# Hybrid attention and SSD layer on one core: the division by the softmax sums moved behind the product with V, and a planner with a transfer limit and averaged times

## The chip, the cores and the metric

The kernel runs on one core of a Trainium2 chip, in one launch. A core has TensorE (PE, with its weight loads shown as PEld), VectorE (DVE), ScalarE (ACT), GpSimd (POOL) and SyncE (SP, which here only issues transfers), each with an instruction stream of its own that runs in order. The metric is the device time of one execution in microseconds (us). Three executions of the kernel before took 977.61, 975.49 and 984.52 us; the median is 977.61 us.

## The reference, cut to what matters

One layer: a modulated RMS norm, one input projection, then latent attention (16 heads) beside a bidirectional Mamba-2 SSD, one output projection, and a gated MLP. The change is about the attention of the latent queries:

```python
def attend(q_nope, q_rope, k_nope, k_rope, v):
    s = (jnp.einsum("bqhd,bkhd->bhqk", q_nope, k_nope)
         + jnp.einsum("bqhr,bkr->bhqk", q_rope, k_rope)) * ATTN_SCALE
    p = jax.nn.softmax(s.astype(jnp.float32), axis=-1).astype(v.dtype)
    return jnp.einsum("bhqk,bkhd->bqhd", p, v)
```

There are 512 latent queries and 768 keys (512 latent, 256 context), and V has 64 columns per head. The softmax divides every row of exponentials by its sum; the product with V is linear, so the division may come before it or after it.

## The kernel before, in words

**Numbers.** Every float32 operand of a large product is split into a high part (`act(..., AF.Copy)`, L498, on ScalarE) and a remainder (`tensor_tensor` subtract, L499, on VectorE), and each product is made of three passes on TensorE (high by high, high by low, low by high).

**Stages, in order of time.** The modulation and the z projection (L685); the other input projections with the depthwise convolution (L752, L787); the SSD of two head groups (L1006 to L1064) beside the attention's projections and, from about 285 us on, beside the attention itself; the attention alone; the output projection (L1299) from about 526 us; its norm and the transposes L1391 at about 600 to 625 us; the MLP's up projection (L752) and the down projection (L1531).

**One unit of attention.** `pair_of_heads(hp, ahead)` does two heads; of each head, four blocks of 128 queries. One block is a unit, 64 units in all. `scores` writes 128 x 768 scores to PSUM with six matmuls (L1176), VectorE takes the row maximum (L1178), ScalarE the exponential into SBUF with the row sum as a second output (L1180), VectorE the reciprocal of that sum, 128 x 1 (L1182), and GpSimd multiplies the 128 x 768 exponentials by it (L1183). Then `transposed` turns the six 128 x 128 blocks on TensorE (L1194), and both remainders and high parts of the transposed block are made by L498 and L499. After two units `weighted` makes the product with V in 24 matmuls (L1206) into the PSUM tile `po`. When a head is done, L1230 and L1231 add the two halves of `po` and write 64 of the 128 rows of `at`, the (value column x query) result of the pair. So in `at` a head is 64 partitions, and a query is a column.

**What else runs on the same engines.** GpSimd also has the SSD's products with per-head factors (L1006 and L1015 in the state steps, L1039, L1045, L1055, L1063), the query rotation (L1126, L1127) and the split of V (L1164). SyncE issues the loads of the weights (L490) and the copies that lay out queries and keys for both heads of a pair (L1151 to L1157). `modfinish` brings a 128 x 8 column table to a row on all partitions: transposed on VectorE (L1273), written to DRAM by four transfers (L1286), and read back by one broadcast (L1288).

**What sets the order.** The program is first written down once; `plan` then gives every instruction a price, simulates five engines and the transfers in `Graph.schedule`, chooses where each SBUF tile lies from the simulated starts and ends, and returns an order of the instructions of each engine, which is then fixed. `plan` repeats this: the starts and ends of one round choose the tiles' places of the next, and the round with the shortest simulated time is kept. A tile that takes the place of another waits for its users. The last four blocks of the output projection's 16 are done in a tail (`keep=4`), and the attention's results stand last in its order, the pair `hp = 7` as the sixteenth block.

## Time and profile before

| | us |
|---|---|
| median of 3 runs | 977.61 |
| profiled execution, its own time | 978.33 |
| its span (first to last instruction) | 976.5 |
| TensorE busy in the span | 952.8 |
| VectorE, ScalarE, GpSimd busy | 775.4, 538.9, 305.0 |
| first and last L1183 start | 294.0, 518.3 |

The span is the time from the first to the last recorded instruction; 1.8 us of the execution's own time lie around it. TensorE's matmuls are pipelined and the ends shown are modelled: a matmul of 512 columns is shown with about 390 ns, while the next one starts some 227 ns later. So a short gap between two matmuls shows as no idle time at all. The share of PEld, the weight loads, tells beside it how densely the matmuls stand.

### The profile page before, as it was taken

The page shows a single profiled execution, that of the slowest core. Times are in us where ns is not written, and L with a number is a line of the kernel's source. Part 1 is how long each engine was busy: PE and PEld are TensorE (multiplying, and loading weights), DVE is VectorE, ACT ScalarE, POOL GpSimd, SP SyncE. Part 2 cuts the span into 40 slices and gives each one's busy share as a digit, 9 for nine tenths or more (in the row PEclk, how much of TensorE's full clock was granted, in tenths as well). Part 3 has the DMA queues.
Part 4 walks back from the last instruction along what each step waited for, and adds up shares of the span by engine and source line. Part 5 has one row for each costly group of instructions (what it writes and reads, how often), then busy time and mean ns, then how long its engine had stood idle before and what let it go on. Part 6 is the DMA issues. An engine that isn't in the chain of part 4 may idle for free. (4 is left out here: it accounts for less than half of the span.)

```text
span 976.5 us, 14760 instructions
## 1 busy us (share of the span) xinstructions
PE 952.8 (98%) x5158; PEld 811.9 (83%) x5158; DVE 775.4 (79%) x1445; ACT 538.9 (55%) x1088; POOL 305.0 (31%) x273
## 2 busy tenths in 40 slices
PE   9999999999989999999999999899999999999995
PEld 8888888889867888898998888788888888887784
DVE  5799858997888999978889987955642542989998
ACT  4455327557669796698897223834412220457673
POOL 0001001874699978466541000000000052230021
PEclk7999999999999999999999999999999999999998
DMA  9913102001241233423487754426334323436784
GB/s 347 385 37 119 54 1 87 1 22 54 68 115 32 72 92 88 106 68 85 120 307 250 253 201 149 162 88 237 108 121 138 107 65 109 151 130 185 254 261 152
DMA packets 50234, 131.34 MB, mean 135 GB/s; under 512 B 6752, under 2 KB 9712, under 8 KB 50160
## 3 DMA queue, kind: packets, MB, share of 16 engines
q1 hardware_dynamic: 49360, 128.72, 41.0%
q10 hardware_dynamic: 800, 1.68, 0.5%
q8 instruction: 41, 0.67, 0.3%
q14 instruction: 33, 0.27, 0.1%
HBM read 110.43 MB, written 4.21 MB: 117 GB/s over the span
## 5 line engine op out<-in xcount | busy, mean ns | idle before, releaser
L752 PE MATMUL banks<-block,block 128*128 128x512 f32 (+1 forms) x2132 | 448.8, 361 | 3.4 <-DVE block L1395 2.0
L752 PEld LDWEIGHTS banks<-block,block 128*128 128x128 f32 x2132 | 358.0, 188 | 64.7 <-DVE block L1395 2.7
L498 ACT ACTIVATE block<-block 128x512 fp32r<-128x512 f32 (+4 forms) x340 | 215.4, 664 | 185.6 <-PE banks L752 48.2
L499 DVE TENSOR_TENSOR block<-block,block 128x512 fp32r<-128x512 f32 (+4 forms) x340 | 265.8, 816 | 50.4 <-PE banks L752 29.2
L1183 POOL TENSOR_TENSOR block<-block,smalls 128x768 f32<-128x768 f32 x64 | 97.1, 1526 | 49.6 <-DVE smalls L1182 32.4
L1531 PE MATMUL banks<-block,block 128*128 128x512 f32 x462 | 108.5, 390 | 1.3 <-DVE block L499 1.1
L1531 PEld LDWEIGHTS banks<-block,block 128*128 128x128 f32 x462 | 86.3, 188 | 21.1 <-DVE block L499 2.5
L1176 PE MATMUL banks<-block,block 128*128 128x512 f32 (+1 forms) x384 | 93.4, 351 | 3.2 <-ACT block L1180 1.7
L499 DVE TENSOR_TENSOR block<-banks,block 128x512 fp32r<-128x512 f32 (+1 forms) x156 | 83.7, 556 | 7.0 <-ACT block L498 5.4
L1299 PE MATMUL banks<-block,block 128*128 128x512 f32 x384 | 89.0, 390 | 0.0
L1299 PEld LDWEIGHTS banks<-block,block 128*128 128x128 f32 x384 | 71.9, 188 | 14.6
L498 ACT ACTIVATE block<-banks 128x512 fp32r<-128x512 f32 (+1 forms) x156 | 74.1, 499 | 16.4 <-PE banks L1194 7.4
L1206 PE MATMUL banks<-block,block 128*128 128x256 f32 x384 | 69.5, 297 | 0.2 <-ACT block L498 0.2
L1176 PEld LDWEIGHTS banks<-block,block 128*128 128x128 f32 x384 | 59.2, 189 | 10.4 <-ACT block L1180 3.5
L587 DVE SCALAR_TENSOR_TENSOR block<-block,block 128x1024 f32<-128x1024 f32 x52 | 62.5, 1219 | 4.9 <-DMA block<-in_wmod_dram 4.9
L1180 ACT ACTIVATE block<-banks,smalls 128x768 f32<-128x768 f32 x64 | 57.8, 904 | 15.5 <-DVE smalls L1178 9.4
L1194 PE MATMUL banks<-cst,block 128*128 128x128 f32 x384 | 63.8, 273 | 0.3 <-DVE block L499 0.2
L1178 DVE TENSOR_REDUCE smalls<-banks 128x1 f32<-128x768 f32 x64 | 60.8, 950 | 3.0 <-PE banks L1176 2.4
L1440 POOL TENSOR_TENSOR block<-block 128x256 f32<-128x256 f32 x11 | 10.4, 952 | 168.4 <-DVE block L1432 143.8
L787 DVE SCALAR_TENSOR_TENSOR block<-banks,cwh,block 128x510 f32<-128x510 f32 (+3 forms) x88 | 51.5, 620 | 12.4 <-ACT block L783 11.9
L1206 PEld LDWEIGHTS banks<-block,block 128*128 128x128 f32 x384 | 56.3, 189 | 4.2 <-ACT block L498 0.6
L1194 PEld LDWEIGHTS banks<-cst,block 128*128 128x128 f32 x384 | 46.8, 140 | 9.0 <-POOL block L1183 1.2
(231 smaller groups left out, 1134.3 us busy)
## 6 DMA issues: line engine op xcount, KB each, us to landing
block<-in_wdn_dram SPq DMA_DIRECT2D x99, 256.0 KB, 3.1
block<-in_wmod_dram SPq DMA_DIRECT2D x48, 512.0 KB, 4.8
block<-in_wup_dram SPq DMA_DIRECT2D x44, 512.0 KB, 3.6
block<-block SPq DMA_DIRECT2D x32, 256.0 KB, 3.1
block<-in_wout_dram SPq DMA_DIRECT2D x16, 512.0 KB, 5.0
block<-block SPq DMA_DIRECT2D x56, 128.0 KB, 2.5
block<-in_wxbc_dram SPq DMA_DIRECT2D x12, 512.0 KB, 4.3
block<-in_wz_dram SPq DMA_DIRECT2D x16, 256.0 KB, 7.3
```

What stands on the lines that cost most here:

```text
L498: act(hi, src, AF.Copy)
L499: (lo_eng or V).tensor_tensor(out=lo, in0=src, in1=hi, op=ALU.subtract)
L587: V.scalar_tensor_tensor(out=junk, in0=wt, scalar=0.5, in1=vec, op0=ALU.mult, op1=ALU.mult, accum_out=acc)
L752: mm(po, lhsT=wf(k, pt[0]), rhs=xf(k, pt[1]), start=(k == 0 and pt == parts[0]), stop=(k == nk - 1 and pt == parts[-1]))
L1176: mm(sc[:, o : o + n], lhsT=q_[:, x_, qi * P : (qi + 1) * P], rhs=kk[:, y_, :], start=part == 0, stop=part == 2)
L1178: V.reduce_max(nm, sc[:, :T], axis=AX.X, negate=True)
L1180: act(pe, sc[:, :T], AF.Exp, bias=nm, scale=1.0, accum_out=sm_)
L1183: G.tensor_tensor(out=pe, in0=pe, in1=sm_.to_broadcast([P, T]), op=ALU.mult)
L1194: nc.tensor.transpose((tx if c < NX else tc_)[:, o : o + P], pe[:, s_ : s_ + P], ident)
L1206: mm(po[:, half * 256 : half * 256 + 256], lhsT=vst(c), rhs=rhs, start=(part == 0 and c == 0), stop=(part == 1 and c == NKT - 1))
L1299: mm(po[i][:, nh * 512 : nh * 512 + 512], lhsT=l[lp][:, i * P : (i + 1) * P], rhs=w[wp][:, nh * 512 : nh * 512 + 512], start=(k == 0 and l ...
L1531: mm(po[i], lhsT=l[:, lp, i * P : (i + 1) * P], rhs=w[wp], start=first and q == 0 and n == 0, stop=q == PAIRS[-1] and n == 2, skip_group_c ...
```

## The change

**In the attention.** `scores` no longer makes the reciprocal (L1182) and no longer multiplies (L1183); what is transposed and multiplied with V are the bare exponentials. The 64 row sums now go to the columns of one tile per pair, `sums` (128 queries x 8 blocks). When both heads of a pair are done, one reciprocal of 128 x 8 is taken, `turned` (taken out of `modfinish`, which uses it too) transposes it on VectorE, four transfers of 8 x 32 elements write it to DRAM as 8 rows of 128, two transfers read four rows each back, each to 64 partitions, and one GpSimd product of 128 x 512 multiplies `at` by it.

**In the planner.** A transfer may not start, in the simulation, before the eighth last one has landed (`FLYING = 8`). The starts and ends that choose the tiles' places are now the mean of the last round's and the new ones. There are 24 rounds, before 16. `PACE = 1.0` only names a number that stood there.

```diff
-DMA_START, DMA_WAIT, DMA_AHEAD, DMA_ALONE, RUN = 650, 910, 3000, 0.8, 80
+DMA_START, DMA_WAIT, DMA_AHEAD, DMA_ALONE, RUN, FLYING = 650, 910, 3000, 0.8, 80, 8
...
-        ticks, held, port = {}, 0, 0.0
+        ticks, held, port, flying = {}, 0, 0.0, []
...
+            if self.dma[i] and not self.back and len(flying) >= FLYING:
+                t = max(t, flying[-FLYING])
...
+            if self.dma[i]:
+                flying.append(end[i] + DMA_WAIT + DMA_ALONE * self.cost[i])
...
-def plan(ins, pieces, hints, units, rounds=16):
+def plan(ins, pieces, hints, units, rounds=24):
...
-        took, order, start, end = Graph(full, eng, dma, cost, share, tables, urgent, opens, shared).best()
+        took, order, *now = Graph(full, eng, dma, cost, share, tables, urgent, opens, shared).best()
+        start, end = ([(p + q) / 2 for p, q in zip(*v)] for v in zip((start, end), now))
...
-    def scores(qkk, qi):
+    def scores(qkk, qi, sum_):
...
-        nm, sm_ = small("nm"), small("rs")
+        nm = small("nm")
         V.reduce_max(nm, sc[:, :T], axis=AX.X, negate=True)
         pe = t4(P, T)
-        act(pe, sc[:, :T], AF.Exp, bias=nm, scale=1.0, accum_out=sm_)
+        act(pe, sc[:, :T], AF.Exp, bias=nm, scale=1.0, accum_out=sum_)
         pfree(sc)
-        V.reciprocal(out=sm_, in_=sm_)
-        G.tensor_tensor(out=pe, in0=pe, in1=sm_.to_broadcast([P, T]), op=ALU.mult)
         return pe, ox, oc
...
+    def turned(w):
+
+        V.transpose(out=w[:, 1, :], in_=w[:, 0, :])
+        return [w[b * 32 : b * 32 + 8, 1, :] for b in range(4)]
+
...
+        sums, inv = t2(P, 2, 32), t2()
+        G.memset(sums[:, 0, 2 * NX :], 0.0)
+        back = nc.dram_tensor(f"sums_{hp}", (2 * NX, P), F32, kind="Internal").ap()
...
-                    transposed(*scores(heads[j], half * 2 + q2), pT, q2)
+                    transposed(*scores(heads[j], half * 2 + q2, sums[:, 0, j * NX + half * 2 + q2 :][:, :1]), pT, q2)
...
+        V.reciprocal(out=sums[:, 0, : 2 * NX], in_=sums[:, 0, : 2 * NX])
+        for b, piece in enumerate(turned(sums)):
+            nc.sync.dma_start(out=back[:, b * 32 : b * 32 + 32], in_=piece)
+        for j in range(2):
+            nc.sync.dma_start(out=inv[j * 64 : j * 64 + 64],
+                              in_=back[j * NX : j * NX + NX].rearrange("(o n) p -> o (n p)", o=1).to_broadcast([64, S]))
+        G.tensor_tensor(out=at, in0=at, in1=inv, op=ALU.mult)
```

TensorE has the same 4977 instructions before and now. VectorE loses 64 reciprocals and gains 8 reciprocals and 8 transposes, GpSimd loses 64 products and gains 8 memsets and 8 products, and SyncE gains 48 transfers. The order of all engines is planned anew. In the changed kernel's order the lines stand 6 higher up to L1176, 4 higher at L1194 and L1206, and 13 higher from L1299 on.

GpSimd, in the SSD's second group, where the decay blocks are made (L1039, now L1045) while attention units run. Before:

```order
L1039 TENSOR_TENSOR block_441_2775<-block_438_2754 128x256
L1183 TENSOR_TENSOR block_387_2529<-block_387_2529,smalls 128x768
L1039 TENSOR_TENSOR block_441_2775<-block_210_1511 128x256
L1045 TENSOR_TENSOR block_438_2754<-block_226_1599,hd 128x512
L1183 TENSOR_TENSOR block_422_2650<-block_422_2650,smalls 128x768
L1039 TENSOR_TENSOR block_441_2775<-block_438_2754 128x256
L1183 TENSOR_TENSOR block_138_806<-block_138_806,smalls 128x768
L1039 TENSOR_TENSOR block_442_2776<-block_210_1511 128x256
```

Now, at the same place:

```order
L1045 TENSOR_TENSOR block_443_2773<-block_427_2685 128x256
L1045 TENSOR_TENSOR block_443_2773<-block_274_1846 128x256
L1045 TENSOR_TENSOR block_443_2773<-block_427_2685 128x256
L1045 TENSOR_TENSOR block_443_2773<-block_274_1846 128x256
L1045 TENSOR_TENSOR block_444_2774<-block_427_2685 128x256
L1132 TENSOR_TENSOR block_274_1846<-block_274_1846,block_106_643 128x512
L1045 TENSOR_TENSOR block_444_2774<-block_274_1846 128x256
L1133 TENSOR_TENSOR block_274_1846<-block_274_1846,block_471_2972 128x512
```

The products with the sums are gone from between the SSD's instructions, and nothing of the attention's units is left on GpSimd there.

TensorE, at the end of the second group's state steps (L1011, now L1017), where the first units' scores (L1176, now L1182) begin. Before:

```order
L1176 MATMUL banks<-block_354_2357,block_201_1425 128x512
L1011 MATMUL banks<-block_43_307,block_208_1504 128x512
L1011 MATMUL banks<-block_43_307,block_209_1505 128x512
L1011 MATMUL banks<-block_59_391,block_208_1504 128x512
L1176 MATMUL banks<-block_29_234,block_201_1425 128x256 x3
L1011 MATMUL banks<-block_31_250,block_208_1504 128x512
L1011 MATMUL banks<-block_31_250,block_209_1505 128x512
L1011 MATMUL banks<-block_43_307,block_208_1504 128x512
L1176 MATMUL banks<-block_354_2357,block_201_1425 128x512 x3
```

Now:

```order
L1182 MATMUL banks<-block_113_674,block_73_460 128x512 x3
L1198 MATMUL banks<-cst,block_277_1899 128x128
L1017 MATMUL banks<-block_295_2001,block_208_1508 128x512
L1017 MATMUL banks<-block_295_2001,block_189_1296 128x512
L1017 MATMUL banks<-block_334_2285,block_208_1508 128x512
L1198 MATMUL banks<-cst,block_277_1899 128x128 x5
L1182 MATMUL banks<-block_356_2364,block_73_460 128x256 x3
L1182 MATMUL banks<-block_113_674,block_73_460 128x512 x2
L1017 MATMUL banks<-block_356_2364,block_208_1508 128x512
```

The first unit's transposes (L1194, now L1198) stood behind the last state product; now those of the first units stand between the state products, with 18 of these still to come when the first transpose is due.

SyncE, where the loads and copies for a coming pair are issued. Before:

```order
L490 DMA block_210_1511<-in_wqr_dram 128x384
L1156 DMA block_642_4149<-block_195_1370 64x1024
L1151 DMA block_72_445<-block_606_3875 64x512
L490 DMA block_616_3933<-in_wk_dram 128x256
L1157 DMA block_43_307<-block_43_307 64x512
L1156 DMA block_59_391<-block_195_1370 64x1024
```

Now, at the first returns of sums (pairs 0 and 2, whose writes alternate; pair 1 follows later):

```order
L1247 DMA sums<-block_210_1514 8x32
L1247 DMA sums<-block_398_2572 8x32
L1163 DMA block_553_3422<-block_43_307 64x512
L1247 DMA sums<-block_210_1514 8x32
L1247 DMA sums<-block_398_2572 8x32
L1249 DMA block_215_1522<-sums 64x512
L496 DMA block_398_2572<-in_wqr_dram 128x384
L1249 DMA block_215_1522<-sums 64x512
L1160 DMA block_611_3867<-block_483_3000 32x1024
L1157 DMA block_611_3867<-block_546_3407 64x1024
```

The writes of the sums and the reads that wait for them stand among the loads and copies for the next pair; behind the first read there stand a weight load and the layout copies. At the end of the output projection, from the sixteen transposes of the first two row blocks to the last four of the fourth, 50 products of the MLP stood between the transposes; now 69 do.

More of the change, by code (lines that the diff above doesn't have):

```diff
@@ L91 @@
 IDLE = 22, 13, 13
+PACE = 1.0
 class Memory:
@@ L1249, in build @@
     second = projections()
-    beside(group_sums(), second, 1.0)
+    beside(group_sums(), second, PACE)
     alone[0] = True
@@ L1266, in modblock @@
         moddot(wt, cs, mod[:, src * 8 + j : src * 8 + j + 1])
-    def row_pieces(ms):
-        w = t2(P, 2, 32)
-        G.memset(w[:, 0, 8:], 0.0)
-        G.tensor_copy(w[:, 0, :8], ms)
-        V.transpose(out=w[:, 1, :], in_=w[:, 0, :])
-        return w[:, 1, :]
     def modfinish(n, src, add, nrm, row=True):
@@ L1283, in modfinish @@
             return
-        turned = row_pieces(ms)
-        for b in range(4):
-            nc.scalar.dma_start(out=scratch[n][:, b * 32 : b * 32 + 32], in_=turned[b * 32 : b * 32 + 8])
+        w = t2(P, 2, 32)
+        G.memset(w[:, 0, 8:], 0.0)
+        G.tensor_copy(w[:, 0, :8], ms)
+        for b, piece in enumerate(turned(w)):
+            nc.scalar.dma_start(out=scratch[n][:, b * 32 : b * 32 + 32], in_=piece)
         row = t4()
```

## The prediction

> **What bounds the kernel now.** The page comes first, for the engines' shares.
>
> ```profile
> span 976.5 us, 14760 instructions
> PE 952.8 (98%) x5158; PEld 811.9 (83%) x5158; DVE 775.4 (79%) x1445; ACT 538.9 (55%) x1088; POOL 305.0 (31%) x273
> ```
>
> TensorE is busy for all but 23.7 us, and the change takes no instruction from it. So the most that any edit of the other engines can win is TensorE's waiting, and the next view must say where that is: the busy time by stage (columns: window, TensorE, weight loads, VectorE, ScalarE, GpSimd, granted clock, DMA share, GB/s).
>
> ```profile
> 0.00:150.00 150.00, 147.76 (x788) 128.69 (x788) 118.62 (x252) 64.13 (x103) 6.40 (x17) 0.95 0.43 157
> 526.00:600.00 74.00, 74.00 (x328) 61.27 (x327) 66.03 (x131) 22.17 (x28) 2.00 (x4) 1.00 0.71 244
> 600.00:625.00 25.00, 21.95 (x141) 19.20 (x140) 22.24 (x80) 18.14 (x49) 1.59 (x1) 1.00 0.51 169
> 625.00:875.00 250.00, 250.00 (x1204) 210.55 (x1204) 138.14 (x184) 83.92 (x120) 38.51 (x46) 1.00 0.37 124
> 875.00:976.50 101.50, 89.86 (x391) 72.59 (x389) 95.37 (x208) 63.79 (x139) 9.54 (x6) 0.97 0.64 207
> ...
> 150.00:293.00 143.00, 138.50 (x786) 116.06 (x784) 123.14 (x193) 94.39 (x209) 88.94 (x73) 1.00 0.20 56
> 293.00:526.00 233.00, 230.73 (x1531) 203.55 (x1532) 211.82 (x404) 192.38 (x446) 158.07 (x127) 1.00 0.39 110
> ```
>
> Nearly half of the idle time, 11.6 us, lies at the end, where the attention is long done, and 2.2 us at the start. The change can reach 4.5 us of 150 to 293, 2.3 us of 293 to 526 and 3.1 us of 600 to 625. Since a short gap shows as no idle time, the same view in finer steps, with a stretch of plain 512-column matmuls as a measure:
>
> ```profile
> 275.00:293.00 18.00, 14.35 (x64) 10.06 (x62) 15.58 (x22) 10.12 (x21) 15.67 (x14) 1.00 0.54 134
> 293.00:350.00 57.00, 55.04 (x343) 45.81 (x344) 52.72 (x92) 46.88 (x127) 52.97 (x45) 1.00 0.25 65
> 350.00:400.00 50.00, 49.99 (x305) 43.27 (x303) 48.82 (x99) 38.01 (x90) 37.24 (x31) 1.00 0.29 72
> 400.00:450.00 50.00, 49.70 (x341) 44.30 (x341) 42.72 (x90) 41.09 (x91) 31.16 (x26) 1.00 0.36 86
> 450.00:526.00 76.00, 76.00 (x549) 70.17 (x548) 67.56 (x126) 66.40 (x141) 36.70 (x27) 1.00 0.59 185
> ...
> 725.00:825.00 100.00, 100.00 (x443) 82.77 (x442) 39.03 (x52) 21.73 (x26) 21.55 (x28) 1.00 0.34 111
> ```
>
> Matmuls that follow each other without a wait keep the weight loads at 83% (725 to 825, wide matmuls) or up to 92% (450 to 526, attention alone, narrow ones). From 275 to 293 they stand at 56%, from 293 to 350 at 80%, then at 87 and 89%. At these two measures the loads of 275 to 293 need 10.06/0.828 = 12.2 us, so 5.8 us are lost; those of 293 to 350 need 49.6 to 55.3, so 1.7 to 7.4 are lost; those of 350 to 450 need 94.9 to 105.8 us of 100, so 0 to 5.1. Together 7.5 to 18.3 us are lost around the first units. There GpSimd is busy for 15.67 of 18 and 52.97 of 57 us, VectorE for 52.72 of 57 and 48.82 of 50. What TensorE waits for in the whole run, where it shows:
>
> ```profile
> PE banks L752 <- DVE block L1395: 2.0, 2, 1.0
> PE banks L1176 <- ACT block L1180: 1.7, 3, 0.9
> PE banks L1176 <- DMA block<-block: 1.5, 2, 1.2
> ```
>
> None of these is GpSimd by name: L1183 stands one step earlier, between a unit's exponential and its transposes.
>
> **The change part by part.** Removed, and the nearest rows to what is added:
>
> ```profile
> L1183 POOL TENSOR_TENSOR block<-block,smalls 128x768 f32<-128x768 f32 x64 | 97.1, 1526 | 49.6 <-DVE smalls L1182 32.4 <-DMA block<-in_wmod_dram 4.0 <-PE banks L1194 2.9
> L1182 DVE RECIPROCAL smalls<-smalls 128x1 f32<-128x1 f32 x64 | 9.4, 156 | 7.4 <-ACT block L1180 6.6
> L1055 POOL TENSOR_TENSOR block<-block,block 128x512 f32<-128x512 f32 x14 | 20.4, 1460 | 5.2 <-DVE block L1053 5.0
> L1271 POOL MEMSET block<- 128x24 f32 x3 | 0.4, 121 | 23.0 <-PE banks L1299 15.4 <-issue 7.6
> L924 DVE RECIPROCAL block<-block 128x192 f32<-128x192 f32 x1 | 1.3, 1346 | 0.0
> L1273 DVE STREAM_TRANSPOSE block<-block 128x32 f32<-128x32 f32 x3 | 0.6, 207 | 0.1
> L1286 ACTq DMA_DIRECT2D mod_rows<-block x12: 269/288/534, 566.6 to 800.8; - x12
> L1288 ACTq DMA_DIRECT2D block<-mod_rows x3: 349/350/353, 576.9 to 927.7; - x3
> block<-block SPq DMA_DIRECT2D x56, 128.0 KB, 2.5
> DMA to landing us min/median/max: 4.7/5.2/5.7
> ```
>
> *GpSimd.* It loses 64 x 1.526 = 97.1 us (its own durations; GpSimd spans are rough) and gains 8 x 1.46 (L1055 is the same shape) and 8 x 0.12, 12.7 us. In 293 to 526 it falls from 158 busy us to about 74. Of itself this is worth nothing: TensorE is the bound, and where other units fill it, the products were hidden. What it is worth is shorter waiting. A unit's way from exponential to transposes loses 0.156 + 1.526 us and, by L1183's idle row, 32.4/64 = 0.5 us of waiting for L1182: about 2.2 us per unit. And the state steps, whose L1006 and L1015 also run on GpSimd, can now be filled with whole units, since a unit needs no GpSimd: in the new order transposes stand between the state products. I take half of the 5.8 us of 275 to 293 (the other half belongs to the SSD's own chain and to the copies of queries and keys, the L1176 row above), 2.9. Of 293 to 350 I take the lower end, 1.7, and 1.0 for all above it, as VectorE stays at over 90% there. Bounds of these: 0, if the idle time is VectorE's, and 18.3.
>
> *VectorE* loses 9.4 us and gains 8 reciprocals of 128 x 8, not in the trace: between 0.156 (one column) and 1.346 (192), taken as 0.2, being near the first; and 8 x 0.207. Net some 6 us less of 212. Its work with both inputs in SBUF also runs beside a freer GpSimd:
>
> ```profile
> L499 DVE TENSOR_TENSOR block<-block,block 128x512 fp32r<-128x512 f32 x14 | 8.8, 687 | 0.0
> L499 DVE TENSOR_TENSOR block<-block,block 128x512 fp32r<-128x512 f32 x34 | 30.5, 900 | 3.5 <-ACT block L498 2.7 <-PE banks L1011 0.5
> ```
>
> The first row is 50 to 125 us, GpSimd nearly idle; the second 150 to 293, GpSimd 62% busy: 0.21 us more for each. This is VectorE time, and counted in the 1.0 above, not once more. Where one reciprocal now waits for the eighth sum, the row maxima behind it on VectorE wait with it: at most the 6.6 us that L1182 waited, in 8 places where it was 17, so nothing is charged.
>
> *The return of the sums.* SyncE gains 32 writes and 16 reads, 32 x 0.288 + 16 x 0.35 = 14.8 us of issuing (ScalarE's rows for the same forms), over some 300 us. A read waits for four writes; behind it stand a weight load and layout copies for the next pair (the order of SyncE). How long a 1 KB write takes to land no row says: at most 3.35 us, as L1288 was issued at 584.45, after its last write at 581.10, and below by nothing but the issue, 0.27.
>
> ```profile
> 581.10 0.27 ACTq L1286 DMA_DIRECT2D mod_rows<-block  x1
> ...
> 584.45 0.35 ACTq L1288 DMA_DIRECT2D block<-mod_rows  x1
> ```
>
> I take 2.5, the landing of the smallest common copy, for the write and 2.5 for the read of 128 KB. The Trainium skill, DMA: Bandwidth & Descriptors, section "Anatomy of one DMA — SWDGE (gpsimd) path", gives a transfer a fixed cost of about 2.0 us, most of it the receipt of the write and heaviest when it goes to HBM, which speaks against a return through DRAM; by it, an estimate from that page, the round trip would be some 4.3 us and the sum no other; the 2.5 us that a 128 KB copy takes here agrees with it. What hides it: nothing needs `at` before the output projection's last blocks. The cover of the last pair is shown by the 526 to 600 row: TensorE runs 74 us without idle time, and the pair is split for its sixteenth block. I charge 0; without the cover the last pair would cost 2.5 + 2.5 + 1.5, 6.5 us, once. On GpSimd the product with the sums waits for the read, and behind it stand splits of V (L1164) for later pairs. SyncE already waits longer than that, in 290 to 526, for what its transfers overwrite or read:
>
> ```profile
> SPq L490 <- PE banks L1194: 27.7, 7, 16.3
> SPq L1151 <- DVE block L499: 29.1, 14, 7.8
> ```
>
> *The planner's edits* move everything else. At 600 to 625, 69 products instead of 50 stand between the transposes.
>
> ```profile
> 616.14 2.43 PE L752 MATMUL banks<-block,block 128*128 128x256 f32 x18
> 618.42 0.60 PE L1391 MATMUL banks<-cst,block 128*128 128x128 f32 x4
> ```
>
> At (618.42 - 616.14)/18 = 0.127 us, 19 more fill 2.4 of the 3.1 idle us, if their operands are there; VectorE, at 22.24 of 25, makes those, so I take 1.0 (bounds 0 and 2.4). Start and end keep their orders but for a few rows: 0.
>
> *Sum:* 2.9 + 1.7 + 1.0 + 1.0 = 6.6 us. The profiled execution took 978.33 us, 0.7 above the median of the runs, 977.61; so 971.0 us.
>
> **The rivals.** About 1% is what a measurement of this kernel can tell from no change: 967.8 and 987.4 us are the bounds.
>
> *Hidden anyway.* The products lay beside TensorE's work, and VectorE, at 92 to 98% from 293 to 400, keeps the first units waiting; the new order loses elsewhere what it wins here. For it: 230.73 of 233 us are already busy. Against it: the weight loads at 56 and 80%. Time 975.5 to 981.
>
> *The whole of it.* All of 18.3 us and some of 2.4 come back, because GpSimd at 93% was what held 293 to 350. Time 977.6 - 18.3 - 1 = 958 at best, 966 at two thirds. For it: state steps and units no longer meet on any engine but VectorE. Against: VectorE.
>
> *Headroom in the weight loads.* They stand at 203.55 of 233 us in the attention; were the rest free, 29.5 us could go: 948. The 92% of 450 to 526 and the 83% of 725 to 825 with no idle time speak against it. The Trainium skill, Perfetto Trace Analysis, section "Identifying the Most-Contended Engine", says matmul busy time is a poor measure of headroom and to take the share of the weight loads; here a stretch without a wait stands at 83%, so the trace follows it only below that.
>
> *SyncE held.* A read of the sums stands at the head of SyncE until four writes land, and the copies of the next pair's queries and keys start late; L1176 then waits for "DMA block<-block", now 1.5 us. Price: 2.5 us (5.2 at the upper landing row) for each of 8 pairs, 20 to 42 us, less the 6.6 won: 991 to 1012; with half the pairs hit, 981. It decides from the point where copies reach SyncE's head less than 2.5 us before their scores. For it: the view shows such waits already. Against: SyncE's waits are for places and for L499, so its loads are mostly early.
>
> **How the numbers follow.** The forecast, 966 to 975.5, has 0.42, of which 0.10 below 967.8; hidden anyway 0.25, same; the whole of it 0.15, faster; headroom 0.03, faster; SyncE held 0.15, of which 0.12 above 987.4. Faster 0.10 + 0.15 + 0.03 = 0.28; slower 0.12; same 0.60. The range 961 to 983 leaves out headroom (0.03), a third of the whole of it (0.05) and most of SyncE held (0.12).
>
> **What would show it.** GpSimd near 220 us in all, no group of 128 x 768 on it; weight loads over 70% in the 18 us around the first scores and over 83% after; L499 of 128 x 512 from SBUF nearer to 687 ns there; 600 to 625 with 1 to 2 us idle. Wrong: VectorE's L499 as TensorE's releaser for more than now; L1176 waiting for copies for over 10 us; idle time in 526 to 600 (the return uncovered); or idle time moved to 875 to 925.

## The result, and the profile after

The changed kernel takes 973.0 us, the median of 20 executions (970.4 to 978.2), beside 977.51 us for the kernel before (20 executions, 975.49 to 984.52). The ratio is 0.995, with a 95% interval of 0.9935 to 0.9965. So the change wins 4.5 us, surely more than nothing and less than the 1% that was set as the bound of "same".

The page of the changed kernel:

```profile
span 976.4 us, 14657 instructions
PE 955.5 (98%) x5158; PEld 816.5 (84%) x5158; DVE 760.4 (78%) x1397; ACT 538.4 (55%) x1088; POOL 224.7 (23%) x225
```

GpSimd went from 305.0 to 224.7 busy us and VectorE from 775.4 to 760.4. But the two profiled spans are equal, 976.5 and 976.4, although the medians differ by 4.5 us. The reason stands in the first 50 us. The kernel before, busy time by window (TensorE, weight loads, VectorE, ScalarE, GpSimd, granted clock, DMA share, GB/s):

```profile
0.00:25.00 25.00, 22.91 (x128) 22.06 (x128) 13.37 (x40) 11.13 (x19) 1.10 (x8) 0.80 0.94 347
25.00:50.00 25.00, 25.00 (x143) 21.91 (x143) 20.33 (x45) 12.05 (x21) 0.00 (x0) 0.93 1.00 379
```

The changed kernel, the same windows:

```profile
0.00:25.00 25.00, 22.97 (x112) 22.41 (x113) 13.36 (x40) 10.89 (x19) 1.10 (x8) 0.70 0.94 344
25.00:50.00 25.00, 25.00 (x136) 22.17 (x135) 15.23 (x36) 7.46 (x13) 0.00 (x0) 0.82 0.87 315
```

The granted clock (third number from the right) was 0.80 and 0.93 in the one execution, 0.70 and 0.82 in the other. In clock time 25 x (0.20 + 0.07) = 6.8 us were lost before and 25 x (0.30 + 0.18) = 12.0 after, 5.2 us more. By then the changed kernel had also done 23 matmuls fewer (112 + 136 for 128 + 143), which at 227 ns each are 5.2 us too. So the profiled execution of the changed kernel, 978.2 us, is its longest of 20, and starts some 5 us behind. The stages behind the start can still be compared, if one keeps in mind that the changed kernel reaches them later.

The rest of the changed kernel by stage, same columns:

```profile
150.00:275.00 125.00, 124.17 (x723) 106.74 (x722) 111.13 (x178) 81.97 (x183) 69.85 (x61) 1.00 0.14 44
275.00:293.00 18.00, 17.32 (x94) 14.01 (x94) 13.50 (x19) 13.74 (x30) 15.81 (x14) 1.00 0.36 85
293.00:350.00 57.00, 55.82 (x361) 47.81 (x360) 52.36 (x91) 47.35 (x122) 35.52 (x35) 1.00 0.32 78
350.00:400.00 50.00, 49.67 (x301) 43.14 (x301) 43.20 (x90) 40.00 (x98) 19.90 (x21) 1.00 0.34 89
400.00:450.00 50.00, 50.00 (x341) 44.42 (x340) 38.35 (x75) 41.30 (x91) 10.39 (x15) 1.00 0.39 97
450.00:526.00 76.00, 75.11 (x531) 67.60 (x530) 68.26 (x115) 63.96 (x134) 10.57 (x12) 1.00 0.67 203
526.00:600.00 74.00, 74.00 (x328) 61.30 (x327) 60.98 (x123) 23.19 (x30) 8.80 (x4) 1.00 0.71 253
600.00:625.00 25.00, 23.61 (x157) 20.91 (x156) 23.35 (x77) 17.21 (x45) 1.29 (x1) 1.00 0.50 175
625.00:875.00 250.00, 250.00 (x1195) 210.23 (x1194) 139.76 (x188) 84.01 (x123) 39.41 (x46) 1.00 0.36 119
875.00:925.00 50.00, 47.83 (x207) 37.94 (x206) 47.92 (x96) 34.11 (x73) 0.00 (x0) 1.00 0.68 211
925.00:976.40 51.40, 40.05 (x177) 32.84 (x175) 45.80 (x110) 29.09 (x64) 8.91 (x6) 0.93 0.62 204
```

The two windows of the kernel before that the prediction does not show:

```profile
150.00:275.00 125.00, 124.16 (x724) 106.00 (x723) 107.56 (x172) 84.27 (x188) 73.27 (x60) 1.00 0.15 45
...
875.00:925.00 50.00, 48.66 (x210) 38.80 (x209) 48.83 (x98) 33.90 (x73) 0.00 (x0) 1.00 0.66 207
```

Both kernels have the same matmuls, so behind the start, where the granted clock is 1.00 in both up to 925 us, the weight loads are an account of work done. (Over the whole span the changed kernel has 4.6 us more of them, 816.5 for 811.9, at the same 5158 loads: those of the first 50 us lasted longer under its lower clock, 180 ns on average for 163, and the 23 that it had not done by 50 us come later.) After minus before, in us:

| stage | weight loads | TensorE idle |
|---|---|---|
| 150 to 275 | +0.74 | -0.01 |
| 275 to 293 | +3.95 | 3.65 to 0.68 |
| 293 to 350 | +2.00 | 1.96 to 1.18 |
| 350 to 526 | -2.58 | 0.31 to 1.22 |
| 526 to 600 | +0.03 | 0 and 0 |
| 600 to 625 | +1.71 | 3.05 to 1.39 |
| 625 to 875 | -0.32 | 0 and 0 |
| 875 to the end | -1.82 | 11.64 to 13.52 |

From 275 to 625 the changed kernel does 5.1 us more of loads in the same 350 us, and 0.7 from 150 to 275. At the rate of that stretch (299.19 us of loads in 350, 0.855) this is 5.8/0.855 = 6.8 us of time. At the end 1.9 us of waiting come back. That leaves 4.9, beside 4.5 by the medians.

What TensorE waits for in the whole of the changed kernel (us, times, longest):

```profile
PE banks L1544 <- DVE block L505: 2.2, 2, 1.5
...
PE banks L758 <- DVE block L1408: 0.7, 2, 0.5
PE banks L1182 <- DMA block<-block: 0.6, 1, 0.6
...
PE banks L1182 <- ACT block L1186: 0.3, 1, 0.3
```

The scores (L1176, now L1182) waited 1.7 us for the exponential and 1.5 for a copy; now 0.3 and 0.6. The transposes' copies (L1395, now L1408) held the MLP's products (L752, now L758) for 2.0 and now for 0.7 us. At the top now is the down projection (L1531, now L1544), waiting 2.2 us near the end for remainders made on VectorE (1.1 before).

What was added, by line (count, then ns min/median/max, first and last start):

```profile
L1245 DVE RECIPROCAL block<-block x8: 194/197/204, 313.7 to 522.8; 128x8 f32<-128x8 f32 x8
L1247 SPq DMA_DIRECT2D sums<-block x32: 267/336/738, 383.8 to 533.7; - x32
L1249 SPq DMA_DIRECT2D block<-sums x16: 450/510/597, 392.8 to 540.1; - x16
L1251 POOL TENSOR_TENSOR block<-block,block x8: 1286/1294/6458, 396.9 to 543.4; 128x512 f32<-128x512 f32 x8
```

And what these wait for in the changed kernel, first GpSimd's group (last part: its idle time ahead of the eight products), then SyncE from 290 to 560 us:

```profile
L1251 POOL TENSOR_TENSOR block<-block,block 128x512 f32<-128x512 f32 x8 | 16.6, 2079 | 80.1 <-DMA block<-sums 68.5 <-DMA block<-block 7.8 <-DVE block L1243 3.7
```

```profile
SPq L1157 <- DVE block L505: 26.0, 15, 7.1
...
SPq L1247 <- DVE block L1215: 12.4, 4, 8.7
...
SPq L1249 <- DMA sums<-block: 9.0, 4, 5.5
```

GpSimd stands 68.5 us ahead of six of the eight products until the sums are back, and SyncE stands 9.0 us until writes have landed. Neither shows on TensorE: 526 to 600 has no idle time, and the scores' wait for copies became shorter.

### The profile page after: what moved, and what is told of

Its sections match the earlier page's. It is cut to its first block, busy times and chain, and to the rows that moved or that the text cites. A ratio compares the mean times of both kernels' runs of the same rounds, so it can differ in the third digit from the quotient of the medians.

```text
span 976.4 us, 14657 instructions
## 1 busy us (share of the span) xinstructions
PE 955.5 (98%) x5158; PEld 816.5 (84%) x5158; DVE 760.4 (78%) x1397; ACT 538.4 (55%) x1088; POOL 224.7 (23%) x225
## 4 chain that ended last, share of the span: by engine, by line
PE 78%; DVE 12%; DMA 4%; issue 3%; ACT 2%; SPq 0%; POOL 0%; DVEq 0%; ACTq 0%; POOLq 0%
PE banks L758 40%; PE banks L1312 7%; DVE block L505 6%; PE banks L691 5%; PE banks L1182 5%; PE banks L1210 4%; PE banks L1198 3%; PE banks L1544 3%; DMA block<-in_wdn_dram 2%; PE banks L1116 2%; DVE block L1537 1%; PE banks L603 1%; DMA block<-block 1%; PE banks L1017 1%; PE banks L1065 1%
## 5 line engine op out<-in xcount | busy, mean ns | idle before, releaser
L758 PE MATMUL banks<-block,block 128*128 128x512 f32 (+1 forms) x2132 | 448.6, 361 | 2.1 <-DVE block L505 0.8
L758 PEld LDWEIGHTS banks<-block,block 128*128 128x128 f32 x2132 | 358.9, 189 | 62.5 <-DVE block L505 1.7
L505 DVE TENSOR_TENSOR block<-block,block 128x512 fp32r<-128x512 f32 (+4 forms) x340 | 262.1, 807 | 34.9 <-ACT block L504 15.8
L1544 PE MATMUL banks<-block,block 128*128 128x512 f32 x462 | 108.4, 391 | 2.2 <-DVE block L505 2.2
L1544 PEld LDWEIGHTS banks<-block,block 128*128 128x128 f32 x462 | 86.2, 188 | 22.1 <-DVE block L505 4.2
L1182 PE MATMUL banks<-block,block 128*128 128x256 f32 (+1 forms) x384 | 95.1, 355 | 0.9 <-DMA block<-block 0.6
L505 DVE TENSOR_TENSOR block<-banks,block 128x512 fp32r<-128x512 f32 (+1 forms) x156 | 83.0, 557 | 9.8 <-ACT block L504 7.8
L1312 PE MATMUL banks<-block,block 128*128 128x512 f32 x384 | 89.4, 391 | 0.0
L504 ACT ACTIVATE block<-banks 128x256 fp32r<-128x256 f32 (+1 forms) x156 | 73.8, 498 | 16.6 <-PE banks L1198 7.3
L1198 PE MATMUL banks<-cst,block 128*128 128x128 f32 x384 | 65.9, 275 | 0.6 <-DVE block L505 0.5
L1182 PEld LDWEIGHTS banks<-block,block 128*128 128x128 f32 x384 | 59.8, 189 | 7.6 <-ACT block L1186 1.3
L1198 PEld LDWEIGHTS banks<-cst,block 128*128 128x128 f32 x384 | 46.5, 140 | 9.1 <-DVE block L505 3.4
L1439 ACT ACTIVATE block<-banks,prm 128x512 f32<-128x512 f32 x22 | 16.8, 776 | 63.9 <-PE banks L758 63.9
L691 PE MATMUL banks<-block,block 128*128 128x512 f32 x192 | 51.7, 421 | 0.0
```

The source lines that it names most:

```text
L504: act(hi, src, AF.Copy)
L505: (lo_eng or V).tensor_tensor(out=lo, in0=src, in1=hi, op=ALU.subtract)
L691: mm(po[i], lhsT=hx[k][:, hp, i * P : (i + 1) * P], rhs=wz[wp], start=(k == 0 and wp == 0 and hp == 0), stop=(k == KD - 1 and hp == 1))
L758: mm(po, lhsT=wf(k, pt[0]), rhs=xf(k, pt[1]), start=(k == 0 and pt == parts[0]), stop=(k == nk - 1 and pt == parts[-1]))
L1182: mm(sc[:, o : o + n], lhsT=q_[:, x_, qi * P : (qi + 1) * P], rhs=kk[:, y_, :], start=part == 0, stop=part == 2)
L1198: nc.tensor.transpose((tx if c < NX else tc_)[:, o : o + P], pe[:, s_ : s_ + P], ident)
```

## The experiments

The explanations at the start were two. By the first the products with the sums cost time where they stood: they lengthened each unit's way and filled GpSimd. By the second they were hidden, and the time changed because all instructions stand in another order. To part them, an order must be held while an instruction goes or comes: the planner is run with the whole program, and the instruction is then taken out of its result (or put in) with all else in its order and its place. The 12 kernels were timed in three groups, each beside the kernel before, whose medians there were 977.89, 977.76 and 976.69 us; ratios are to those.

**The order before, without the products.**

```diff
-        V.reciprocal(out=sm_, in_=sm_)
-        G.tensor_tensor(out=pe, in0=pe, in1=sm_.to_broadcast([P, T]), op=ALU.mult)
+        if not PLANNED[0]:
+            mark = here()
+            V.reciprocal(out=sm_, in_=sm_)
+            G.tensor_tensor(out=pe, in0=pe, in1=sm_.to_broadcast([P, T]), op=ALU.mult)
+            MARKS.append((mark, here()))
...
+    order = {e: [new[i] for i in l if i in new] for e, l in order.items()}
```

> The kernel before with its order of every engine and its tile places kept, but the 64 reciprocals and the 64 GpSimd products of 128 x 768 left out (the output lacks the division by the sums). Theory A, the products cost time where they stand: 2 to 5 us less than the kernel before, 972.5 to 975.5, with TensorE's idle time in 275 to 350 (5.6 us before) down by at least 2. Theory B, the products are hidden and the new order is what is worth the time: within 1.5 us of the kernel before, 976 to 979.

Measured: 976.97 us, ratio 0.999, 0.9973 to 1.0007. Its windows around the first units:

```profile
275.00:293.00 18.00, 14.17 (x64) 9.91 (x62) 15.64 (x23) 10.43 (x22) 15.70 (x14) 1.00 0.54 133
293.00:350.00 57.00, 55.25 (x347) 46.29 (x348) 48.81 (x77) 46.76 (x126) 29.00 (x31) 1.00 0.25 64
```

GpSimd fell from 52.97 to 29.00 us in 293 to 350, and TensorE's numbers are the kernel before's within 0.5 us: 14.17 for 14.35, 55.25 for 55.04; loads 9.91 for 10.06, 46.29 for 45.81. All 64 products and reciprocals together cost 0.9 us at the most likely and 2.6 at the most (0.0027 x 977). The products were hidden under the order before, and TensorE's idle time from 275 to 350, which the first explanation had down by at least 2 us, stays at 5.6: the first explanation falls.

**The order after, with a product put back.** Every unit has a 128 x 768 GpSimd product by ones between its exponential and its transposes, at the place in GpSimd's order that the plan's times give.

```diff
         act(pe, sc[:, :T], AF.Exp, bias=nm, scale=1.0, accum_out=sum_)
+        if PLANNED[0]:
+            MARKS.append(here())
+            G.tensor_tensor(out=pe, in0=pe, in1=ones[:, :1].to_broadcast([P, T]), op=ALU.mult)
         pfree(sc)
```

> The changed kernel with its order and tile places kept, and one GpSimd product of 128 x 768 by a column of ones put back between each unit's exponential and its transposes (the same GpSimd time and the same wait as before the change, without the reciprocal). Theory A: 3 to 8 us more than the changed kernel, 976 to 981, since the order has no room for it. Theory B: at most 1.5 us more, 973 to 974.5.

Measured: 1004.44 us, ratio 1.027, 1.0243 to 1.0296; 31 us over the changed kernel, more than either explanation had. Its windows:

```profile
293.00:350.00 57.00, 49.39 (x298) 40.92 (x298) 47.23 (x67) 40.36 (x103) 45.42 (x40) 0.97 0.24 60
350.00:400.00 50.00, 41.31 (x244) 34.33 (x245) 47.26 (x75) 34.84 (x89) 31.79 (x28) 1.00 0.30 78
```

What TensorE waits for most in it, and the group of the new products:

```profile
PE banks L1204 <- DVE block L508: 10.3, 11, 1.8
```

```profile
L1192 POOL TENSOR_TENSOR block<-block,ones 128x768 f32<-128x768 f32 x64 | 102.5, 1602 | 67.3 <-ACT block L1189 62.0 <-DMA block<-block 2.0 <-PE banks L1204 1.4
```

TensorE loses 7.6 us from 293 to 350 and 8.7 from 350 to 400, although GpSimd is busy for no more than 45.42 of 57 us there. By name its transposes (L1204 in this run) wait 10.3 us for remainders made on VectorE (L508). So what an instruction costs is no property of the instruction: the order before had room for the 64 products, the order after has none at the places where they were put. Whether other places on GpSimd would have been cheaper was not tried.

**Each half of the change alone.** First the attention's edit with the planner before (mean and limit taken out, 16 rounds):

```diff
-            if self.dma[i] and not self.back and len(flying) >= FLYING:
-                t = max(t, flying[-FLYING])
...
-def plan(ins, pieces, hints, units, rounds=24):
+def plan(ins, pieces, hints, units, rounds=16):
...
-        took, order, *now = Graph(full, eng, dma, cost, share, tables, urgent, opens, shared).best()
-        start, end = ([(p + q) / 2 for p, q in zip(*v)] for v in zip((start, end), now))
+        took, order, start, end = Graph(full, eng, dma, cost, share, tables, urgent, opens, shared).best()
```

> The attention part of the change alone: sums applied after the product with V, planner as before (no limit, no averaging, 16 rounds). Theory A: 971 to 975, most of the gain. Theory B: 976 to 979, no gain.

Measured: 976.81 us, ratio 0.9989, 0.9969 to 1.0008. Then the planner's edits with the attention before:

```diff
-    def scores(qkk, qi, sum_):
+    def scores(qkk, qi):
...
+        V.reciprocal(out=sm_, in_=sm_)
+        G.tensor_tensor(out=pe, in0=pe, in1=sm_.to_broadcast([P, T]), op=ALU.mult)
```

> The planner part of the change alone: attention as before, with the limit of 8, the averaged times and 24 rounds. Theory A: 976 to 979, no gain. Theory B: 971 to 975, most of the gain.

Measured: 978.37 us, ratio 1.0013, 0.9996 to 1.0029. Neither half alone can be told from no change; together they give 0.995. But the attention's edit alone does change what TensorE does. Its profiled execution, beside the kernel before (275 to 350 and 350 to 526 us), first the attention's edit alone:

```profile
275.00:350.00 75.00, 72.01 (x443) 61.30 (x442) 67.46 (x115) 59.69 (x153) 46.35 (x45) 1.00 0.31 77
350.00:526.00 176.00, 174.73 (x1158) 153.87 (x1157) 146.35 (x272) 142.08 (x312) 38.19 (x46) 1.00 0.50 138
```

The kernel before:

```profile
275.00:350.00 75.00, 69.39 (x407) 55.87 (x406) 68.30 (x113) 57.00 (x146) 68.64 (x58) 1.00 0.32 81
350.00:526.00 176.00, 175.69 (x1191) 157.74 (x1190) 159.10 (x313) 145.50 (x320) 105.10 (x83) 1.00 0.44 125
```

Around the first units the loads rise by 5.43 us, nearly as in the changed kernel (61.82, 5.95 more), and from 350 to 526 they fall by 3.87 (2.58 in the changed kernel). So the old planner finds the better filling of 275 to 350 as well, and gives more of it back from 350 on; in that execution the granted clock was also 0.93 from 600 to 625, 1.7 us of clock time. Of the planner's edits only the averaged times do anything: with the limit of eight transfers left out, or with 16 rounds, the changed kernel's instructions get the same order and the same places. What is left of the second explanation is narrower: not any new order, but the orders that instructions without the 64 products allow, and among these not every one.

**Where the 31 us of the product put back come from.** Two 128 x 256 products per unit that nobody reads, so that GpSimd has its in-order work but no unit waits for it:

```diff
+        if PLANNED[0]:
+            MARKS.append(here())
+            G.tensor_tensor(out=junk_, in0=pe[:, :256], in1=ones[:, :1].to_broadcast([P, 256]), op=ALU.mult)
+            MARKS.append(here())
+            G.tensor_tensor(out=junk_, in0=pe[:, 512:], in1=ones[:, :1].to_broadcast([P, 256]), op=ALU.mult)
```

> The changed kernel with its order and tile places kept, and two GpSimd products of 128 x 256 per unit put back whose result nobody reads (about the same GpSimd time as the old product, but no unit waits for it). If the 31 us of the product by one were GpSimd's time: 990 us or more. If they were the unit's wait (exponential, product, transposes in a row): 973 to 977.

Measured: 989.24 us, ratio 1.0118, 1.0088 to 1.0147; 16 us over the changed kernel: near the 990 us expected if GpSimd's time were the cause, and far from the 973 to 977 of the other case. Its window, and the first of the two groups:

```profile
293.00:350.00 57.00, 51.04 (x311) 42.34 (x310) 47.01 (x74) 41.40 (x106) 45.23 (x53) 0.97 0.26 63
```

```profile
L1193 POOL TENSOR_TENSOR junkp<-block,ones 128x256 f32<-128x256 f32 x64 | 46.3, 724 | 65.4 <-ACT block L1190 65.3
```

GpSimd stands 65.3 us before these products until the exponential of their unit is done, and what is queued behind them waits with it; 18.8 us of this lie between 275 and 400, where the SSD still runs and where TensorE loses most. So about half of the 31 us is GpSimd's queue and the other half, by difference, the units' own longer way. The difference is not clean: the two products of a unit took 87.9 us of GpSimd in all (46.3 and 41.6) where the product by ones took 102.5, and they also hold the exponentials' buffers a little longer; how much that is was not measured.

**The order after, without the return of the sums.**

```diff
+        if not PLANNED[0]:
+            mark = here()
+            V.reciprocal(out=sums[:, 0, : 2 * NX], in_=sums[:, 0, : 2 * NX])
...
+            G.tensor_tensor(out=at, in0=at, in1=inv, op=ALU.mult)
+            MARKS.append((mark, here()))
```

> The changed kernel with its order and tile places kept, but the return of the sums left out: the 8 reciprocals of 128 x 8, their transposes, the 48 transfers and the 8 products of 128 x 512 (the output lacks the division). If the return is hidden, as the prediction has it: 972 to 974. If SyncE or GpSimd is held by it: 2 us less or more, below 971.

Measured: 971.73 us, ratio 0.9937, 0.9908 to 0.9967. Beside the changed kernel's 973.0 the reciprocals, transposes, 48 transfers and 8 products cost 1.3 us at the most likely; the two intervals overlap, so it can't be told from nothing. The end of this kernel's attention and of its down projection:

```profile
526.00:600.00 74.00, 74.00 (x328) 61.29 (x327) 59.58 (x126) 21.21 (x27) 2.29 (x2) 1.00 0.67 232
...
900.00:925.00 25.00, 23.43 (x100) 18.19 (x99) 22.43 (x47) 16.38 (x35) 0.00 (x0) 1.00 0.75 237
```

526 to 600 is as with the return, so the last pair's return is covered. And 1.6 us of idle time from 900 to 925 are here too, so that what the end gives back belongs to the order, not to the sums.

**Other orders of the same instructions.** A round of the planner gives an order, and the planner keeps the one with the shortest simulated time. Four kernels take the order of another round instead: two with the instructions of the changed kernel, two with those of the kernel before.

```diff
-        if found is None or took < found[0]:
+        if _ == 23:
             found = took, places, order
```

> The same instructions as the changed kernel, but the order and places of another of the planner's rounds, the twenty-fourth. Theory C, the two parts need each other (a unit without GpSimd leaves room, averaged times use it), holds for orders in general: 971.5 to 975.5. Theory D, one order among many happened to be good: 976 to 981, as for the attention part under the old planner (976.8).

Measured: 979.85 us, ratio 1.0017, 1.0 to 1.0033. That is where theory D, one good order among many, had it.

```diff
-        if found is None or took < found[0]:
+        if _ == 7:
             found = took, places, order
```

> The kernel before with the order and places of another round of its planner, the eighth. It shows how far orders of the same instructions lie apart: theory C, within 2 us of the kernel before, 975.5 to 980; theory D, 3 us or more away to either side.

Measured: 984.67 us, ratio 1.0065, 1.004 to 1.009: orders of the same instructions do not lie within 2 us of each other. The next pair takes round 6 of each:

> The instructions of the changed kernel in the order and places of the planner's seventh round. With the twenty-fourth round's at 979.9, theory E expects it between the two, 973 to 980; theory D the same, but below 972 would speak against D.

> The instructions of the kernel before in the order and places of its planner's seventh round; the eighth's took 984.7. Theory E: 978 to 986, above the kernel before. Theory D: anywhere in 972 to 986, as likely below 977.5 as above.

Measured: 986.64 us, ratio 1.0097, 1.0069 to 1.0125, for the changed kernel's instructions, and 991.28 us, ratio 1.0144, 1.011 to 1.0178, for those before. Both lie outside what was expected. The same instructions come to times that lie 14 us apart; that is three times what the change wins. These four are orders that the planner itself ranked behind the one it kept, so the 14 us are no scatter among equally good choices. Part of it is clock time. In the slowest order, 991.28 us, the granted clock falls below 1.00 in the middle of the kernel as well:

```profile
275.00:300.00 25.00, 20.30 (x86) 14.65 (x85) 21.60 (x29) 13.03 (x28) 22.84 (x19) 0.93 0.49 113
600.00:650.00 50.00, 46.12 (x251) 40.17 (x250) 44.81 (x127) 28.29 (x63) 1.27 (x1) 0.93 0.41 135
```

These are some 5 us of clock time (25 x 0.07 + 50 x 0.07) in that execution; the kernel before and the changed one have 1.00 in both places. Why the clock fell there is not shown.

**Another mean in the planner, new and old attention.** If the 4.5 us were one lucky draw, other weights of the mean should lose them; if instructions without the products have better orders, the new attention should win again and the old one should not.

```diff
-        start, end = ([(p + q) / 2 for p, q in zip(*v)] for v in zip((start, end), now))
+        start, end = ([(2 * p + q) / 3 for p, q in zip(*v)] for v in zip((start, end), now))
```

> The changed kernel with one number of the planner changed: the times that choose the tiles' places are two thirds the last round's and one third the new ones, so another order and other places. Theory E, orders scatter by several us, units without GpSimd have better ones, and the planner can find them: 968 to 974, as good as the changed kernel or better. Theory D, the changed kernel's order is one lucky draw: 975 to 981.

Measured: 969.37 us, ratio 0.9918, 0.9894 to 0.9941: the fastest of all, 3.6 us below the changed kernel, though its interval and that of the changed kernel (0.9935 to 0.9965) still touch. That is where theory E had it, and below all that theory D had. The old attention had the wider search: of some 250 orders of its instructions, made with several weights and rounds, the one with the shortest simulated time.

```diff
-        start, end = ([(p + q) / 2 for p, q in zip(*v)] for v in zip((start, end), now))
+        start, end = ([(p + 2 * q) / 3 for p, q in zip(*v)] for v in zip((start, end), now))
```

> The attention as before (product on GpSimd in each unit), with the order that the planner ranks best among some 250 that it made with several weights of the mean. Theory E: no order of the old attention comes down to the changed kernel, 975 to 979. Theory D: a draw as good as the changed kernel's is found, 970 to 974.

Measured: 975.58 us, ratio 0.9994, 0.9976 to 1.0012, again within theory E's 975 to 979 and above theory D's 970 to 974. The windows of the new attention with that mean:

```profile
293.00:350.00 57.00, 56.50 (x372) 49.14 (x370) 52.23 (x104) 50.42 (x137) 31.84 (x34) 1.00 0.26 67
...
600.00:625.00 25.00, 24.26 (x180) 22.79 (x180) 24.50 (x75) 21.28 (x51) 1.47 (x1) 1.00 0.33 113
```

And of the old attention in its best order:

```profile
293.00:350.00 57.00, 55.18 (x355) 47.51 (x355) 54.60 (x91) 48.00 (x128) 53.40 (x44) 1.00 0.27 69
350.00:400.00 50.00, 48.03 (x283) 40.31 (x282) 45.04 (x102) 36.94 (x89) 38.38 (x32) 1.00 0.31 76
```

With the new attention the loads reach 49.14 of 57 us and 22.79 of 25 (86 and 91%). The old one comes to 47.51 in 293 to 350 with VectorE at 54.60 and GpSimd at 53.40 of 57, and then loses 2 us from 350 to 400.

**All orders together**, by ratio:

| | best | second | third | fourth | fifth |
|---|---|---|---|---|---|
| new attention | 0.9918 | 0.995 | 0.9989 | 1.0017 | 1.0097 |
| old attention | 0.9994 | 1 | 1.0013 | 1.0065 | 1.0144 |

Rank by rank the new attention is better by 0.0076, 0.005, 0.0024, 0.0048 and 0.0047, about half a per cent. Five orders of each, picked by hand, are few, and in the whole time the two scatter over each other: that the better ranks are no accident is likely, not shown.

In one stage they do not scatter over each other. The weight loads of TensorE in us, one profiled execution of each order, in the sequence of the table above:

| | best | second | third | fourth | fifth |
|---|---|---|---|---|---|
| new attention, 275 to 350 | 62.13 | 61.82 | 61.30 | 61.03 | 60.91 |
| old attention, 275 to 350 | 58.67 | 55.87 | 58.57 | 55.97 | 57.00 |
| new attention, 350 to 526 | 155.66 | 155.16 | 153.87 | 151.57 | 146.92 |
| old attention, 350 to 526 | 152.84 | 157.74 | 153.44 | 153.72 | 150.69 |

The lowest of the new and the highest of the old, in 275 to 350:

```profile
275.00:350.00 75.00, 72.97 (x445) 60.91 (x444) 66.88 (x105) 56.34 (x138) 51.62 (x47) 1.00 0.32 80
...
275.00:350.00 75.00, 70.59 (x427) 58.67 (x426) 71.29 (x113) 58.61 (x150) 69.83 (x58) 1.00 0.28 71
```

Around the first units every order without the 64 products is filled better than every order with them, under either planner; the old instructions in their fixed order with the products left out stay at 56.20 (9.91 + 46.29). So this part of the gain belongs to the instructions and needs a new order to come out. What the orders of the new attention differ in is how much they lose elsewhere: from 350 to 526 us their loads fall in the sequence in which their times rise. The old attention's show no such sequence.

Shown is, then, that the products taken away win nothing in a fixed order, that the planner's edits win nothing for the old instructions, that the orders without the products fill 275 to 350 better, and that no order tried of the old instructions, the best-planned one among them, comes near 0.995. Not shown is why the averaged times give an order that loses less elsewhere.

## Why the prediction was right, and where it was off

The time was forecast at 971.0 in a range of 961 to 983, and "same" at 0.60; 973.0 with a gain of 4.5 us is that case, and the forecast's own range, 966 to 975.5, holds it too. The steps:

- **The bound: TensorE's waits around the first units and from 600 to 625.** Right. These are the places where the account of loads rises: +3.95, +2.00 and +1.71 us.
- **2.9 us of 275 to 293.** Too small: the loads rose from 56 to 78% of the window, 3.95/0.828 = 4.8 us, most of the 5.8 that were taken for lost. "Over 70%" came true. The last state matmul also starts later now (301.8 us for 294.3), of which some 5 us are the longer start and the rest, by difference, the units between the matmuls; so the windows do not hold quite the same stage.
- **1.7 us of 293 to 350.** About right: 2.00/0.828 = 2.4 us, loads at 84%, "over 83%".
- **1.0 us for all above that, up to 450.** About 0.7 of it came, in 293 to 350 (2.4 for 1.7); from 350 to 450 nothing did (87.57 and 87.56 us of loads). VectorE's relief came there (48.82 to 43.20 and 42.72 to 38.35 us), but TensorE had next to no idle time (0.31 us).
- **450 to 526, taken as full and put at nothing.** Wrong: the loads fell from 70.17 to 67.60 and 0.9 us of idle time came up. That is 2.57 us of loads, some 2.9 us of time at the 90% of 350 to 526 (157.74 of 176 before).
- **1.0 us of 600 to 625.** Too small: the loads rose by 1.71 us, idle time fell by 1.7 to 1.39, inside the "1 to 2". It need not be the attention's: two orders of the old attention have loads of 20.69 and 21.64 us there (the planner's edits alone, and the best order), for 19.20 before.
- **"Start and end keep their orders but for a few rows: 0."** With 450 to 526 this is the step that failed: the end gave back 1.9 us of waiting, 0.8 of it in 875 to 925 (1.34 idle before, 2.17 now), the rest around and behind the last matmuls. The same waiting from 900 to 925 in the run without the return shows that it is the order's.
- **The return of the sums at 0.** Held within what can be measured: 1.3 us at the most likely, indistinguishable from none. Its parts were near: the reciprocal 0.197 us (0.2 taken), the writes' issue 0.336 (0.288 taken), the reads' 0.51 (0.35 taken), the GpSimd product 1.294 at the median (1.46 taken; one of the eight took 6.458). GpSimd came to 224.7 us, 220 forecast. The transfers' way was put too short. For the last pair, the fourth write, the reads and the product:

```profile
533.68 0.35 SPq L1247 DMA_DIRECT2D sums<-block  x1
539.64 1.09 SPq L1249 DMA_DIRECT2D block<-sums  x2
...
543.36 6.46 POOL L1251 TENSOR_TENSOR block<-block,block 128x512 f32<-128x512 f32 x1 [28.77 <-DMA block<-sums]
```

From the last write's issue to the product 9.7 us passed where 5.0 were taken, and the read stood 5.5 us for the write, more than the 3.35 that was taken for the most. It was hidden all the same: 526 to 600 has no idle time.
- **VectorE's operations from SBUF nearer to 687 ns beside a freer GpSimd.** Half right; the two groups of the changed kernel, 150 to 293 and 293 to 526:

```profile
L505 DVE TENSOR_TENSOR block<-block,block 128x512 fp32r<-128x512 f32 x32 | 29.4, 929 | 6.1 <-ACT block L504 4.1 <-PE banks L1017 1.1 <-POOL block L1045 0.7
...
L505 DVE TENSOR_TENSOR block<-block,block 128x512 fp32r<-128x512 f32 x21 | 16.7, 804 | 0.4 <-ACT block L504 0.3
```

In 150 to 293, where GpSimd is as busy as before, 929 ns stand for 900; from 293 on, where it was freed, 804 (925 before). That is what the step said of the cause, but it is no gain, as the points above on 350 to 526 show.

The sum of terms, 6.6 us, met 6.8 us in the middle, by larger gains at 275 to 293 and 600 to 625 and a loss between, so that the two sums agree is luck; the 1.9 us at the end, charged at nothing, make the difference to what was measured.

Of the signs of being wrong two came true. Idle time did move to 875 to 925 (1.34 to 2.17 us). And TensorE waits more for the remainders made on VectorE (L499, now L505), 3.5 us in the longer waits of the whole run for 2.4, by the down projection at the end; from 275 to 530 it is 0.5 for 1.3. The other two, over 10 us of waiting for copies and idle time from 526 to 600, did not.

What the prediction did not see is how the gain comes about. "What it is worth is shorter waiting", so many us per unit, is not so: with the order held, the units' way 1.7 us shorter (1.526 + 0.156) and GpSimd freed, TensorE's waits stayed as they were (the first experiment). The other half of that sentence, that state steps can be filled with whole units since a unit needs no GpSimd, is the one that fits the runs: all five orders of the new attention fill 275 to 350 better than all five of the old, and with the planner without the averaged times that filling came too, but not the gain in time, as more was lost elsewhere.

**The rivals.** "Hidden anyway" was right in its first half, that the products were hidden, and wrong in its second, that the new order would lose elsewhere what it won: it lost a part of it, some 2.9 us from 350 to 526 and 1.9 at the end. "The whole of it" did not come; no order came below 969.37 us. "Headroom in the weight loads" did not either: no stage shown here rose above 91%, and the mark from 450 to 526 was 92%. "SyncE held": a read does stand at SyncE's head until the writes land, 9.0 us in 4 cases, 5.5 at the longest, but the scores' wait for copies fell to 0.6 us, since the copies come early enough.

## What to carry to other kernels

Here work that hid on a filler engine cost no time in a fixed order, but it took freedom from the order; so judge such a removal twice, once with the order held and once planned anew, and expect the gain only from the second. Where a planner orders a kernel, the scatter among its own orders can be larger than an edit is worth (here 14 to 17 us for the same instructions, against 4.5), so compare several orders of both versions before an edit is believed, stage by stage and not in the total alone, and try a few settings of the planner beside it: one other weight of the mean, at 969.37 us, won 3.6 us more beside the change's 4.5. And charge an edit that plans everything anew with something for the stages that it does not touch.

## What was not expected of the hardware

TensorE's granted clock at the start is not the same from one execution to the next, with the same instructions in the same order there. The run with the product by ones has the changed kernel's order, and its first 50 us were:

```profile
0.00:25.00 25.00, 23.06 (x132) 22.28 (x133) 13.37 (x40) 10.98 (x19) 1.11 (x8) 0.80 0.94 354
25.00:50.00 25.00, 25.00 (x141) 21.79 (x141) 20.86 (x45) 12.04 (x21) 0.00 (x0) 0.93 0.99 369
```

It had 0.80 and 0.93 and 273 matmuls, where the profiled execution of the changed kernel had 0.70 and 0.82 and 248. The clock is not all of it: the run with the dead products, in the same order, had 0.80 and 1.00 and also 273. The 5.2 us of clock time between the two profiles at the top are as large as the change, and those two profiles alone would have shown no gain at all.

Small work on an in-order engine with time to spare was dear: 64 pairs of products of 0.65 to 0.72 us whose results nobody reads cost 16 us, with GpSimd busy for 45.23 of 57 us at the worst place. Ahead of them its queue stood 18.8 us for operands between 275 and 400 us, with the SSD's instructions behind.
